# A two-layer decoder trunk on one core: low rank and decays one chunk later, pooling's sums put off behind the tile's two evacuations, three early weight splits in place of six

## The chip, the cores and the metric

The kernel runs on one core of a Trainium2 chip, in one launch. The metric is device time in microseconds (us) of that core, as the median of several runs. The kernel before has a median of 1512.12 us (1510.86, 1512.12, 1513.85).

## The reference

The input x has 2048 tokens of width 1024. Two layers follow each other; each projects x by one wide matrix, runs two groups of heads, gates them with SiLU, maps back by an output matrix, adds 1.41 x and normalises.

```python
def _even_layer(...):
    h = x @ w_in
    q, k, v, g_a, a_lr, u, sv, g_b = _split(h, EVEN_SIZES)
    log_a = jax.nn.log_sigmoid((a_lr @ w_a2 + b_a)) / GLA_TAU        # rank 16
    o = _gla(q, k, v, log_a)              # gated linear attention, 4 heads, chunks of 64
    o_a = _head_rmsnorm(o, gla_norm_g) * jax.nn.silu(g_a)
    o_b = _spatial_gating(jax.nn.gelu(u), jax.nn.gelu(sv), ...) * jax.nn.silu(g_b)
    return _layer_norm(DN_ALPHA * x + jnp.concatenate([o_a, o_b], -1) @ w_out, ln_g, ln_b)

def _odd_layer(...):
    q, k, v, g_c, p, g_d = _split(x @ w_in, ODD_SIZES)
    o = _retention(rotary(q), rotary(k), v)                         # 4 heads, chunks of 128
    o_c = _head_groupnorm(o, ret_norm_g) * jax.nn.silu(g_c)
    o_d = _multiscale_pool(p, w_pool, pool_scale) * jax.nn.silu(g_d)  # windows 2, 4, 8, 16
    return _layer_norm(DN_ALPHA * x + jnp.concatenate([o_c, o_d], -1) @ w_out, ln_g, ln_b)
```

`_multiscale_pool` takes, per group of 128 channels, the mean of the last w tokens minus the token itself, and multiplies it by a 128 x 128 matrix.

## The kernel before, in words

The tokens are worked through in four blocks of 512; each block goes through layer 0 and then layer 1, so every weight is read four times. All large products are made of fp32r pairs: `split` (L87 to L90) cuts a tile into a high part (a copy on ACT, L89) and a low part (a subtraction on DVE, L90), and each 128 x 128 weight tile is multiplied in three passes (high by high, high by low, low by high).

**Units.** `unit` computes one group of 512 output columns (or 256, 272) from eight tiles of 128 rows each (`kt`). It does two of the four outputs at a time, in two PSUM buffers of the pool `big`, which has four. So the matmuls of the second pair run while the first pair is evacuated by `evac`. A unit has 96 matmuls. The first unit of the first block alone does all four outputs at once (`width=4`).

**Weights.** SP fetches weights in order into `raw` (seven buffers); `cut` splits the next landed one into one of twelve `wt` buffers. `pace` is called after each `kt` and lets a cut through whenever its credit reaches 1.0. Where a unit needs a tile that isn't cut yet, it cuts it on the spot.

**Steps.** Work that isn't part of a unit is put in a list by `later(fn, delay)`. `between` is called four times in a unit (after a quarter of its matmuls each; here a chunk); it lowers every delay by one and runs what has reached zero, in the order of the list. The order on each engine is the order in which the program calls; nothing is moved afterwards.

**The start of a block** (`layer0`). Unit 1 gives half of v and the 16 columns of the low rank: `evac_v0` copies these to `alr` (DVE, L502 to L504) and v to `vt` (eight copies by `values`, L370 on ACT; in the first block half of them L373 on DVE). Unit 2 (256 columns) gives the rest of v. Meanwhile three steps follow one another: `low_rank` (four transposes L511, the copy `alrT` L512), `decay` (two matmuls L455, then L458 to L464 on ACT and L459 on DVE) and `decay2` (the scan and the exponentials, L471 to L485, with `f` at L522 to L524). Unit 3 gives q and k; its `evac_qk` multiplies them by the decays (L549, L550) after the first pair, and two chunks later PE transposes the keys (L555).

**Pooling** (`layer1`, `pool_unit`). Its first pair of outputs are two channel groups of p, its second pair their gates. Evacuating p copies the 16 carried tokens (L785, DVE) and the tile (L786, ACT) into `pb`, adds shifted copies (L791; one to four additions), scales (L796), saves the carry (L799) and splits the result. After the second pair, `out` multiplies it by the pooling matrix (L778, PE) in a PSUM buffer of the pool `trp`, which has two. The retention's steps (`attend`, L385 on PE; L413, L417, L733, L752 on DVE) run in the same units; their state products sit in `trp` too.

```python
later(low_rank, 1)
later(decay, 2)
later(decay2, 3)
...
pace(3 * width * cols / 512.0 if width < 4 else 0.75 * 6)
...
credit[0] = min(credit[0] + matmuls / 6.0, 2.0)
while credit[0] >= 1.0 and room[0] > hold[0] and landed:
    cut()
    credit[0] -= 1.0
```

Of the kernel before, what the change touches and what calls it, by code (L numbers as in the profile page):

```python
# [9 lines left out]
F32 = mybir.dt.float32  # L10
# [3 lines left out]
ALU = mybir.AluOpType  # L14
# [3 lines left out]
P = 128  # L18
# [3 lines left out]
TB = 512  # L22
NB = SEQ // TB
# [3 lines left out]
WINDOWS = (2, 4, 8, 16)  # L27
# [24 lines left out]
def trunk(ctx, tc, x, xT, pos, wv, w, w_a2, pvec, rowp, sgu_rows, w_sT, w_pool, ropec, poolc, out):  # L52
    nc = tc.nc
# [10 lines left out]
    pl = ctx.enter_context(tc.tile_pool(name="pl", bufs=4))  # L64
# [9 lines left out]
    def big():  # L74
        return ps_big.tile([P, 512], F32, tag="big", name="big")

    def tr():
        return ps_tr.tile([P, 4, P], F32, tag="tr", name="trp")

    def w2(name):  # L80
        return work.tile([P, TB], F32, tag="w2", name=name)

    def flat(t):
        return t.rearrange("p a b -> p (a b)")


    def split(src, hi, lo):  # L87

        nc.scalar.activation(hi, src, AF.Copy)  # L89
        nc.vector.tensor_tensor(lo, src, hi.bitcast(F32), op=ALU.subtract)  # L90
# [23 lines left out]
    def cut():  # L114
        raw, n, width = landed.pop(0)
        assert room[0] > 0
        room[0] -= 1
        t = wpool.tile([P, 2, 512], F32R, tag="w", name="wt")
        c = n * width
        split(raw[:, 0:c], t[:, 0, 0:c], t[:, 1, 0:c])  # L120
        ready.extend((t[:, :, i * width:(i + 1) * width], i == n - 1) for i in range(n))
        fetch()

    def pace(matmuls):
# [4 lines that stand above are left out]
# [9 lines left out]
    def act_unit():  # L138
        return acts.tile([P, 4, 2, TB], F32R, tag="T", name="T")
# [4 lines left out]
    def later(fn, delay=1):  # L144
        steps.append([delay, fn])

    def between():
        ready = []
        for e in steps:
            e[0] -= 1  # L150
            if e[0] <= 0:
                ready.append(e)
        for e in ready:
            steps.remove(e)
        for e in ready:
            e[1]()
# [7 lines left out]
    def unit(xs, evac, token_major, width=2, cols=512):  # L164


        wt = []
        for n in range(0, 4, width):
            ps = [big()[:, 0:cols] for _ in range(width)]
            for kt in range(KT):  # L170
                if len(wt) == kt:
                    while not ready:
                        cut()
                    wt.append(ready.pop(0))
                t, last = wt[kt]
                for i, p_ in enumerate(ps):
                    sl = slice((n + i) * P, (n + i + 1) * P)
                    xt = xs[kt // 4][:, kt % 4]
                    for q, (a, b) in enumerate(PASSES):
                        lhsT, rhs = (xt[:, a, sl], t[:, b, :]) if token_major else (t[:, a, sl], xt[:, b, :])  # L180
                        nc.tensor.matmul(p_, lhsT=lhsT, rhs=rhs, start=(kt == 0 and q == 0),  # L181
                                         stop=(kt == KT - 1 and q == 2))
                if n + width == 4 and last:
                    room[0] += 1
                pace(3 * width * cols / 512.0 if width < 4 else 0.75 * 6)
                if width > 1 and (kt + 1) % (KT // width) == 0 and kt < KT - 1:
                    between()
            for i, p_ in enumerate(ps):
                evac(n + i, p_)
            between()  # L190
# [12 lines left out]
    def gate(dst_u, h, psT, gain, sil):  # L203

        y = w2("y")
        nc.vector.scalar_tensor_tensor(y, psT, gain, sil, op0=ALU.mult, op1=ALU.mult)  # L206
        later(lambda: split(y, dst_u[:, h, 0, :], dst_u[:, h, 1, :]))

    def layer_norm_out(xs, rows, lnrow, after, cuts=1):
        ln = r8.tile([P, 2, D], F32, tag="r8", name="ln")  # L210
        for i in range(2):
            nc.sync.dma_start(ln[:, i, :], rowp[lnrow + i:lnrow + i + 1, :].broadcast_to([P, D]))
        gt, bt = ln[:, 0, :], ln[:, 1, :]
        sts = [small.tile([P, 2, 6], F32, tag="lnst", name="lnst", bufs=5) for _ in range(NT)]

        def evac(half, t, ps):
            row = rows[t // 2][:, t % 2, :]
            rh = row[:, half * 512:half * 512 + 512]
            nc.vector.scalar_tensor_tensor(rh, rh, ALPHA, ps, op0=ALU.mult, op1=ALU.add)  # L219
            nc.vector.bn_stats(sts[t][:, half, :], rh)  # L220
            if half == 1:
                mv = small.tile([P, 2], F32, tag="lnmv", name="lnmv")
                nc.vector.bn_aggr(mv, sts[t])  # L223
                rs = small.tile([P, 1], F32, tag="lnrs", name="lnrs")
                rstd(rs, mv[:, 1:2], LN_EPS)

                def scale():
                    nc.vector.scalar_tensor_tensor(row, row, mv[:, 0:1], gt, op0=ALU.subtract, op1=ALU.mult)  # L228
                    for c in range(0, D, D // cuts):
                        cs = slice(c, c + D // cuts)  # L230
                        nc.vector.scalar_tensor_tensor(row[:, cs], row[:, cs], rs, bt[:, cs],  # L231
                                                       op0=ALU.mult, op1=ALU.add)
                        after(t, row, cs)

                later(scale)

        unit(xs, lambda t, ps: evac(0, t, ps), True)
        unit(xs, lambda t, ps: evac(1, t, ps), True, width=1)
# [25 lines left out]
    carry = const.tile([P, 4, 16], F32, name="carry")  # L264
# [8 lines left out]
    poolt = const.tile([P, 4, 16], F32, name="poolt")  # L273
# [14 lines left out]
    for kt in range(KT):  # L288
# [3 lines left out]
        raw, _, width = landed.pop(0)  # L292
# [195 lines left out]
    def layer0(b, xs):  # L488
# [6 lines left out]
        def values(t, ps, s):  # L495
            by_heads(both_copy if b == 0 and s == 0 else act_copy,
                     lambda r, c: vt[half(r), t, (2 * c + s) * P:(2 * c + s + 1) * P],
                     lambda c, r: ps[half(c), r * P:(r + 1) * P])
# [29 lines left out]
        if b == 0:  # L528
            constants()
            later(constants2, 3)  # L530
            later(constants3, 4)
        later(low_rank, 1)
        later(decay, 2)
        later(decay2, 3)
        unit(xs, lambda t, ps: values(t, ps, 1), True, cols=256)


# [149 lines left out]
    def layer1(b, xs, rows):  # L687
# [76 lines left out]
        cc, cd = act_unit(), act_unit()  # L764


        def pool_unit(half):
            def evac(n, ps):
                g = 2 * half + n % 2
                slot = (g + 2) % 4  # L770
                if n >= 2:
                    sg = w2("sg")
                    nc.scalar.activation(sg, ps, AF.Silu)

                    def out():
                        pt = flat(tr())
                        for n, (i, j) in enumerate(PASSES):
                            nc.tensor.matmul(pt, lhsT=wp[:, i, g * P:(g + 1) * P], rhs=cd[:, slot, j, :],  # L778
                                             start=(n == 0), stop=(n == 2))
                        gate(cd, slot, pt, pool_s[:, g:g + 1], sg)  # L780

                    later(out, 1)
                    return
                pb = pl.tile([P, 16 + TB], F32, tag="pl", name="pb")
                nc.vector.tensor_copy(pb[:, 0:16], carry[:, g, :])  # L785
                nc.scalar.activation(pb[:, 16:], ps, AF.Copy)  # L786
                src, off, step = pb, 0, 1
                while step < WINDOWS[g]:
                    off2 = off + step
                    dst = pl.tile([P, 16 + TB], F32, tag="pl", name="pl")  # L790
                    nc.vector.tensor_tensor(dst[:, off2:], src[:, off2:], src[:, off2 - step:16 + TB - step], op=ALU.add)  # L791
                    src, off, step = dst, off2, step * 2
                if b == 0:
                    nc.gpsimd.tensor_tensor(src[:, 16:32], src[:, 16:32], poolt[:, g, :], op=ALU.mult)
                pd = w2("pd")
                nc.vector.scalar_tensor_tensor(pd, src[:, 16:], 1.0 / WINDOWS[g], pb[:, 16:],  # L796
                                               op0=ALU.mult, op1=ALU.subtract)
                if b < NB - 1:
                    nc.vector.tensor_copy(carry[:, g, :], pb[:, TB:TB + 16])  # L799

                split(pd, cd[:, slot, 0, :], cd[:, slot, 1, :])

            unit(xs, evac, False)

        pool_unit(1)
# [110 lines left out]
```

## Time and profile before

| what | value |
|---|---|
| median of 3 runs | 1512.12 us |
| the profiled execution: its time / its span | 1510.03 us / 1508.3 us |
| PE busy with matmuls | 1472.0 us, 98% of the span, 8752 matmuls |
| PE idle | 36.3 us |
| DVE busy | 985.4 us, 65% |
| ACT busy | 594.9 us, 39% |
| mean DMA traffic | 108 GB/s |
| mean granted clock of PE | 0.993 |

Of the chain that ended last, PE holds 84%, and 76% of the span is the line of the large products, L181. PE has little idle time, so what matters is where it idles, what ended each wait, and in which stretches its clock was granted at half.

### The profile page before, as it was taken

The page shows a single profiled execution, that of the slowest core. Times are in us where ns is not written, and L with a number is a line of the kernel's source. Part 1 is how long each engine was busy: PE and PEld are TensorE (multiplying, and loading weights), DVE is VectorE, ACT ScalarE, POOL GpSimd, SP SyncE. Part 2 cuts the span into 40 slices and gives each one's busy share as a digit, 9 for nine tenths or more (in the row PEclk, how much of TensorE's full clock was granted, in tenths as well). Part 3 has the DMA queues.
Part 4 walks back from the last instruction along what each step waited for, and adds up shares of the span by engine and source line. Part 5 has one row for each costly group of instructions (what it writes and reads, how often), then busy time and mean ns, then how long its engine had stood idle before and what let it go on. Part 6 is the DMA issues. An engine that isn't in the chain of part 4 may idle for free.

```text
span 1508.3 us, 23315 instructions
## 1 busy us (share of the span) xinstructions
PE 1472.0 (98%) x8752; PEld 1226.2 (81%) x8752; DVE 985.4 (65%) x2008; ACT 594.9 (39%) x1116; POOL 116.3 (8%) x185
## 2 busy tenths in 40 slices
PE   7999999999999999999999999999999999999997
PEld 6888888788878888878887888887888888888786
DVE  5596486756657458675665746867575564696655
ACT  5634324243643333434264342333427434143430
POOL 1020010100101001000100100000010010100001
PEclk9999999999999999999999999999999999999999
DMA  7324423124523341313352344232435225222321
GB/s 235 98 69 156 122 74 111 58 70 156 168 84 102 124 140 56 113 57 113 127 168 87 97 135 116 63 106 70 137 111 160 86 84 169 83 91 78 92 83 56
DMA packets 87059, 162.35 MB, mean 108 GB/s; under 512 B 10097, under 2 KB 18337, under 8 KB 86945
## 3 DMA queue, kind: packets, MB, share of 16 engines
q1 hardware_dynamic: 86944, 160.85, 34.3%
q8 instruction: 69, 1.13, 0.3%
q14 instruction: 46, 0.37, 0.1%
HBM read 152.43 MB, written 8.39 MB: 107 GB/s over the span
## 4 chain that ended last, share of the span: by engine, by line
PE 84%; DVE 6%; ACT 4%; issue 2%; DMA 1%; POOL 1%; SPq 1%; DVEq 0%; POOLq 0%; ACTq 0%
PE big L181 76%; PE att L385 3%; DVE wt L90 2%; ACT v L370 1%; DVE pl L791 1%; PE trp L778 1%; PE trp L626 1%; PE trp L678 1%; ACT wt L89 1%; PE trp L385 1%; DMA raw<-in_wv 1%; DVE ta L472 0%; SPq L109 0%; PE trp L718 0%; PE trp L814 0%
## 5 line engine op out<-in xcount | busy, mean ns | idle before, releaser
L181 PE MATMUL big<-wt,T 128*128 128x512 f32 (+2 forms) x3456 | 727.0, 370 | 10.9 <-DVE v L373 6.4
L181 PEld LDWEIGHTS big<-wt,T 128*128 128x128 f32 x3456 | 600.1, 190 | 117.8 <-ACT v L370 6.8
L181 PE MATMUL big<-T,wt 128*128 128x512 f32 x2688 | 630.6, 393 | 5.6 <-ACT v L370 5.6
L181 PEld LDWEIGHTS big<-T,wt 128*128 128x128 f32 x2688 | 501.7, 188 | 116.1 <-ACT v L370 8.6
L90 DVE TENSOR_TENSOR wt<-raw,wt 128x512 fp32r<-128x512 f32 (+1 forms) x496 | 318.0, 672 | 247.3 <-ACT wt L89 246.0
L89 ACT ACTIVATE wt<-raw 128x512 fp32r<-128x512 f32 (+1 forms) x496 | 296.3, 615 | 327.4 <-PE big L181 236.2
L219 DVE SCALAR_TENSOR_TENSOR rows<-rows,big 128x512 f32<-128x512 f32 x64 | 43.6, 681 | 59.0 <-PE big L181 59.0
L198 POOL TENSOR_SCALAR lnrs<-lnmv 128x1 f32<-128x1 f32 x32 | 33.3, 1042 | 615.8 <-DVE lnmv L223 615.8
L370 ACT ACTIVATE v<-big 64x128 f32<-64x128 f32 (+1 forms) x184 | 56.6, 308 | 35.0 <-PE big L181 17.7
L680 ACT ACTIVATE T<-trp 128x512 fp32r<-128x512 f32 x32 | 17.4, 596 | 106.5 <-PE trp L678 106.5
L231 DVE SCALAR_TENSOR_TENSOR rows<-rows,lnrs,ln 128x1024 f32<-128x1024 f32 (+1 forms) x36 | 41.6, 1165 | 19.5 <-POOL lnrs L201 18.6
L201 POOL TENSOR_TENSOR rs<-rs,neghalf 128x4 f32<-128x4 f32 x48 | 49.3, 1028 | 3.9
L220 DVE BATCH_NORM_STATS2 lnst<-rows 128x6 f32<-128x512 f32 x64 | 44.4, 694 | 2.2
L228 DVE SCALAR_TENSOR_TENSOR rows<-rows,lnmv,ln 128x1024 f32<-128x1024 f32 x32 | 41.0, 1282 | 0.9
L206 DVE SCALAR_TENSOR_TENSOR y<-trp,pv,sg 128x512 f32<-128x512 f32 x48 | 33.7, 744 | 9.5 <-PE trp L653 5.3
L786 ACT ACTIVATE pb<-big 128x512 f32<-128x512 f32 x16 | 9.4, 590 | 74.4 <-PE big L181 74.4
L89 ACT ACTIVATE T<-y 128x512 fp32r<-128x512 f32 x48 | 29.4, 627 | 23.6 <-DVE y L206 23.2
L638 ACT ACTIVATE act<-big 128x512 f32<-128x512 f32 x32 | 18.3, 596 | 51.2 <-PE big L181 50.5
L604 DVE BATCH_NORM_STATS2 st<-zt 128x6 f32<-128x128 f32 x64 | 13.6, 275 | 35.0 <-ACT zt L600 35.0
L791 DVE TENSOR_TENSOR pl<-pb 128x527 f32<-128x527 f32 x16 | 11.3, 708 | 32.6 <-ACT pb L786 31.8
L90 DVE TENSOR_TENSOR T<-y,T 128x512 fp32r<-128x512 f32 x48 | 31.6, 688 | 0.5
L744 DVE BATCH_NORM_STATS2 st<-att 128x6 f32<-128x128 f32 x64 | 14.2, 284 | 22.4 <-PE att L385 21.9
(197 smaller groups left out, 981.4 us busy)
## 6 DMA issues: line engine op xcount, KB each, us to landing
raw<-in_w SPq DMA_DIRECT2D x448, 256.0 KB, 2.9
xraw<-in_xT SPq DMA_DIRECT2D x32, 256.0 KB, 3.6
rows<-in_x SPq DMA_DIRECT2D x8, 1024.0 KB, 7.6
ln<-in_rowp SPq DMA_DIRECT2D x16, 512.0 KB, 6.1
out<-rows SPq DMA_DIRECT2D x12, 512.0 KB, 2.7
raw<-in_wv SPq DMA_DIRECT2D x32, 136.0 KB, 3.0
raw<-in_wv SPq DMA_DIRECT2D x32, 128.0 KB, 2.9
out<-rows SPq DMA_DIRECT2D x8, 256.0 KB, 2.0
```

The costliest lines, as they stand in the source:

```text
L89: nc.scalar.activation(hi, src, AF.Copy)
L90: nc.vector.tensor_tensor(lo, src, hi.bitcast(F32), op=ALU.subtract)
L181: nc.tensor.matmul(p_, lhsT=lhsT, rhs=rhs, start=(kt == 0 and q == 0), stop=(kt == KT - 1 and q == 2))
L198: nc.gpsimd.tensor_scalar(dst, var, eps, None, op0=ALU.add)
L201: nc.gpsimd.tensor_tensor(dst, dst, neghalf[:, :n], op=ALU.pow)
L206: nc.vector.scalar_tensor_tensor(y, psT, gain, sil, op0=ALU.mult, op1=ALU.mult)
L219: nc.vector.scalar_tensor_tensor(rh, rh, ALPHA, ps, op0=ALU.mult, op1=ALU.add)
L220: nc.vector.bn_stats(sts[t][:, half, :], rh)
L228: nc.vector.scalar_tensor_tensor(row, row, mv[:, 0:1], gt, op0=ALU.subtract, op1=ALU.mult)
L231: nc.vector.scalar_tensor_tensor(row[:, cs], row[:, cs], rs, bt[:, cs], op0=ALU.mult, op1=ALU.add)
L370: nc.scalar.activation(dst, src, AF.Copy)
L385: nc.tensor.matmul(dst, lhsT=lhsT, rhs=rhs, start=start, stop=stop, skip_group_check=True)
```

## The change

Three edits, word for word:

```diff
-                pace(3 * width * cols / 512.0 if width < 4 else 0.75 * 6)
+                pace(3 * width * cols / 512.0 if width < 4 else 2.4)
...
-        later(low_rank, 1)
-        later(decay, 2)
-        later(decay2, 3)
+        later(low_rank, 2)
+        later(decay, 3)
+        later(decay2, 4)
...
                 pb = pl.tile([P, 16 + TB], F32, tag="pl", name="pb")
                 nc.vector.tensor_copy(pb[:, 0:16], carry[:, g, :])
                 nc.scalar.activation(pb[:, 16:], ps, AF.Copy)
-                src, off, step = pb, 0, 1
-                while step < WINDOWS[g]:
...
-                split(pd, cd[:, slot, 0, :], cd[:, slot, 1, :])
+
+                def sums():
+                    src, off, step = pb, 0, 1
+                    while step < WINDOWS[g]:
...
+                    split(pd, cd[:, slot, 0, :], cd[:, slot, 1, :])
+
+                later(sums)
```

The body of `sums` is the old code, unchanged. In the changed file the lines of the pooling sums are two higher (L793 for L791, L798 for L796, L801 for L799), and so are those of the second transposes, L818 for L814.

How it moves instructions is shown at three places.

**ACT, start of the first block**, from the last splits ahead of unit 1's evacuation (`v` is the tile of values, `alrT` the low rank; the eight copies are those of two outputs' evacuations). Before:

```order
L89 ACTIVATE wt<-raw 128x512 x6
L370 ACTIVATE v_232<-big 64x128 x8
L89 ACTIVATE wt<-raw 128x512 x2
L512 ACTIVATE alrT<-trp 48x512
```

Now:

```order
L89 ACTIVATE wt<-raw 128x512 x3
L370 ACTIVATE v_232<-big 64x128 x8
L89 ACTIVATE wt<-raw 128x512 x4
L370 ACTIVATE v_232<-big 64x128 x8
L512 ACTIVATE alrT<-trp 48x512
L89 ACTIVATE wt<-raw 128x512 x2
L89 ACTIVATE wp<-wraw 128x512
L458 ACTIVATE ta<-trp,pv 128x512 x2
L462 ACTIVATE ta<-ta 128x512 x2
L464 ACT_TABLE_LOAD
L464 ACTIVATE ta<-ta 128x512 x2
L89 ACTIVATE wt<-raw 128x512 x2
```

Three splits stand ahead of the first evacuation in place of six, and eleven in place of twelve ahead of the exponentials; the twelfth is the eighth weight tile of unit 3.

**ACT, start of the second block**, the same steps (`G` are the scaled q and k):

```order
 L370 ACTIVATE v_3695<-big 64x128 x8
-L89 ACTIVATE wt<-raw 128x512 x2
+L89 ACTIVATE wt<-raw 128x512 x3
+L370 ACTIVATE v_3695<-big 64x128 x8
 L512 ACTIVATE alrT<-trp 48x512
-L89 ACTIVATE wt<-raw 128x512
-L370 ACTIVATE v_3695<-big 64x128 x8
+L89 ACTIVATE wt<-raw 128x512 x2
 L458 ACTIVATE ta<-trp,pv 128x512 x2
```

```order
 L89 ACTIVATE wt<-raw 128x512 x2
+L370 ACTIVATE v_3695<-big 64x128 x8
 L482 ACT_TABLE_LOAD
```

The low rank now stands behind unit 2's first evacuation and one more split, and unit 2's second evacuation has moved from behind the exponentials to ahead of them. On PE the four transposes L511 move behind 24 more matmuls, and so do the two L455.

**DVE, the pooling of two channel groups, first block** (`pb` is the tile with its carry, `pl` the sums, `pd` the result). Before:

```order
L785 COPY pb<-carry 128x16
L791 TENSOR_TENSOR pl<-pb 128x527
L791 TENSOR_TENSOR pl<-pl 128x525
L791 TENSOR_TENSOR pl<-pl 128x521
L796 SCALAR_TENSOR_TENSOR pd<-pl,pb 128x512
L799 COPY carry<-pb 128x16
L90 TENSOR_TENSOR T<-pd,T 128x512
L785 COPY pb<-carry 128x16
```

Now:

```order
L785 COPY pb<-carry 128x16 x2
L793 TENSOR_TENSOR pl<-pb 128x527
L793 TENSOR_TENSOR pl<-pl 128x525
L793 TENSOR_TENSOR pl<-pl 128x521
L798 SCALAR_TENSOR_TENSOR pd<-pl,pb 128x512
L801 COPY carry<-pb 128x16
L90 TENSOR_TENSOR T<-pd,T 128x512
```

Only the second group's carry copy has moved, ahead of the first group's sums; the sums themselves stand where they stood, since `between` follows the evacuations at once and a delay of one is then spent.

## Rows read from the trace of the kernel before

**Rows 1.** The page: span, and busy time by engine.

```profile
span 1508.3 us, 23315 instructions
...
PE 1472.0 (98%) x8752; PEld 1226.2 (81%) x8752; DVE 985.4 (65%) x2008; ACT 594.9 (39%) x1116; POOL 116.3 (8%) x185
```

**Rows 2.** What PE waited for, whole span: us in total, times, longest us.

```profile
PE trp L778 <- DVE s L417: 9.5, 4, 2.8
PE big L181 <- DVE v L373: 6.4, 2, 5.7
PE big L181 <- ACT v L370: 5.6, 6, 1.7
...
PE trp L455 <- ACT alrT L512: 1.6, 3, 0.5
```

**Rows 3.** Timeline, first block: start, us, engine, line, tiles, count, idle before.

```profile
17.74 0.69 DVE L90 TENSOR_TENSOR wt<-raw,wt 128x512 fp32r<-128x512 f32 x1 [0.79 <-ACT wt L89]
...
23.22 0.16 DVE L502 CAST alr<-big 128x16 fp32r<-128x16 f32 x1
...
25.01 0.98 PE L181 MATMUL big<-wt,T 128*128 128x256 f32 x3 [5.65 <-DVE v L373]
...
26.70 4.33 PE L181 MATMUL big<-wt,T 128*128 128x256 f32 x21 [0.71 <-DVE v L373]
...
34.90 6.01 PE L181 MATMUL big<-wt,T 128*128 128x256 f32 x48
36.30 1.26 ACT L458 ACTIVATE ta<-trp,pv 128x512 f32<-128x512 f32 x2
...
41.56 16.88 PE L181 MATMUL big<-T,wt 128*128 128x512 f32 x72
...
50.04 1.14 ACT L89 ACTIVATE wt<-raw 128x512 fp32r<-128x512 f32 x2
```

**Rows 4.** Stretch after that wait: busy by engine, granted clock, DMA share, GB/s.

```profile
25.00:30.20 5.20, 4.48 (x19) 4.22 (x20) 3.16 (x16) 2.53 (x8) 0.00 (x0) 0.50 0.70 229
```

**Rows 5.** Timeline, start of the second block.

```profile
399.32 1.16 PE L511 MATMUL trp<-ident,alr 128*48 128x128 f32 x4
...
402.06 1.15 ACT L89 ACTIVATE wt<-raw 128x512 fp32r<-128x512 f32 x2
...
403.88 0.73 PE L455 MATMUL trp<-alrT,wa 48*128 48x512 f32 x2 [0.53 <-ACT alrT L512]
...
410.40 11.07 PE L181 MATMUL big<-T,wt 128*128 128x512 f32 x48
...
421.99 2.25 ACT L370 ACTIVATE v<-big 64x128 f32<-64x128 f32 x8
422.81 0.68 DVE L549 TENSOR_TENSOR G<-big,ta 128x512 f32<-128x512 f32 x1
423.15 0.96 PE L181 MATMUL big<-T,wt 128*128 128x512 f32 x3 [1.68 <-ACT v L370]
...
429.19 0.60 PE L555 MATMUL trp<-ident,G 128*128 128x128 f32 x4
```

**Rows 6.** Timeline, pooling in the first block.

```profile
279.95 0.17 DVE L785 COPY pb<-carry 128x16 f32<-128x16 f32 x1
...
291.31 1.63 PE L778 MATMUL trp<-T,wp 128*128 128x512 f32 x6 [2.83 <-DVE s L417]
292.78 5.64 PE L181 MATMUL big<-T,wt 128*128 128x512 f32 x24
```

**Rows 7.** Timeline, the same place in the second block.

```profile
661.59 2.76 PE L778 MATMUL trp<-T,wp 128*128 128x512 f32 x6 [2.23 <-DVE s L417]
664.14 6.10 PE L181 MATMUL big<-T,wt 128*128 128x512 f32 x24
```

**Rows 8.** Stretches behind both pooling waits, columns as in rows 4.

```profile
291.30:298.30 7.00, 6.99 (x30) 5.53 (x30) 5.84 (x12) 1.78 (x4) 0.00 (x0) 1.00 0.44 134
...
661.90:665.10 3.20, 3.20 (x9) 2.46 (x9) 3.16 (x8) 0.57 (x2) 0.00 (x0) 0.50 0.00 0
```

More of the change, by code (lines that the diff above doesn't have):

```diff
@@ L786, in evac @@
                 nc.scalar.activation(pb[:, 16:], ps, AF.Copy)
-                src, off, step = pb, 0, 1
-                while step < WINDOWS[g]:
[L789 to L799, printed above, removed]
-                split(pd, cd[:, slot, 0, :], cd[:, slot, 1, :])
+                def sums():
+                    src, off, step = pb, 0, 1
+                    while step < WINDOWS[g]:
+                        off2 = off + step
+                        dst = pl.tile([P, 16 + TB], F32, tag="pl", name="pl")
+                        nc.vector.tensor_tensor(dst[:, off2:], src[:, off2:], src[:, off2 - step:16 + TB - step], op=ALU.add)
+                        src, off, step = dst, off2, step * 2
+                    if b == 0:
+                        nc.gpsimd.tensor_tensor(src[:, 16:32], src[:, 16:32], poolt[:, g, :], op=ALU.mult)
+                    pd = w2("pd")
+                    nc.vector.scalar_tensor_tensor(pd, src[:, 16:], 1.0 / WINDOWS[g], pb[:, 16:],
+                                                   op0=ALU.mult, op1=ALU.subtract)
+                    if b < NB - 1:
+                        nc.vector.tensor_copy(carry[:, g, :], pb[:, TB:TB + 16])
+                    split(pd, cd[:, slot, 0, :], cd[:, slot, 1, :])
+                later(sums)
             unit(xs, evac, False)
```

## The prediction
> **What bounds the kernel now.** I read the page first: PE is busy for 1472.0 of 1508.3 us [rows 1], so no other engine sets the time by its load, and the change, which takes no matmul away, can only earn what PE idles or runs slowly: 36.3 us of idle time, and stretches at half clock. Second, the waits of PE over the whole span [rows 2]. Four of them stand where this change moves something: the pooling matmuls behind DVE (9.5 us in four waits, one a block), the first block's second unit behind evacuation copies on DVE (6.4), q and k's second pair behind evacuation copies on ACT (5.6 in six, two in each later block), and the decay matmuls behind the low rank (1.6 in three). Third, the timeline at each of these places, to see what the releasing engine did just before. Fourth, the granted clock behind the waits, since a wait can cost more than its length.
>
> In the first block DVE finishes the third early split at 18.43 (17.74 + 0.69), but takes up the first evacuation only at 23.22, behind splits four to six; PE idles 5.65 us until 25.01 and 0.71 more until 26.70 [rows 3]. In that stretch the granted clock is 0.50, that is 1.2 of 2.4 GHz [rows 4], and 21 matmuls take 4.33 us where 48 later ones take 6.01, 0.125 us each [rows 3]. In the second block the wait for ACT is 1.68 us at 423.15: ACT frees those buffers with eight copies only from 421.99, behind the exponentials [rows 5].
>
> **Early splits.** With three, DVE is free at 18.43. The first output's last matmul should be done by then (an estimate: unit 1 ends 5.65 us before 25.01, at 19.36; the other three outputs' last nine matmuls, at some 0.15 us, come after it). So evacuation starts at about 18.45 in place of 23.22, 4.8 us earlier, and PE resumes at about 20.2, takes the second buffer at 21.9, and has idled 0.9 and 1.3 us in place of 6.36.
>
> Does the clock still fall? The nearest rows disagree. Behind a pooling wait of 2.83 us the clock stayed at 1.00, behind one of 2.23 us it was 0.50 for some three us [rows 8]. The price of a fall is 1.6 us: six and 24 matmuls took 2.76 + 6.10 in place of 1.63 + 5.64 [rows 6, 7]. For about 2.2 us of idling cut in two I take the dearer end, that it falls. The Trainium skill ("TensorE: Matmul & The Clock Gate", the two states) says that the hardware's watch on the engine runs freely and doesn't restart with the kernel, so that the same kernel shows a different number of slow matmuls from run to run; the two pooling waits agree with that, and by it this term could be 1 us better.
>
> The three splits left out are not gone; they move behind the evacuation, and the chain of the decays has to be crossed before the twelfth. At the slow clock 21 matmuls end at 26.2 (21.9 + 4.33); 24 more at 0.125 at 29.3; then eight copies (2.25, as in [rows 5]), the low rank (about 0.6, as for one split), two splits (1.15) and wp's (0.6) bring L458 to 33.9, against 36.30. From L458 to the first split behind the exponentials it was 13.74 us (36.30 to 50.04) [rows 3]; I keep that and get 47.6, and 48.2 when its high part is done. PE meanwhile: 24 matmuls 3.0, the decays' two 0.7 [rows 5], 24 more 3.0, and, as estimates, 0.4 for the transposes without their wait and 0.8 for the eight small ones of a constant bias give 37.2 for the start of q and k, against 41.56. A tile takes six matmuls of 0.234 (16.88 / 72), so the eighth is wanted at 47.0 and PE stalls for about 1.2 us, some 1.5 with its low part. The first pair ends near 49.9 in place of 52.8 (41.56 + 48 x 0.234): **minus 2.9**. At the full clock it is minus 3.9 with a stall of 2.0. The bounds are minus 4.8 (no stall) and nothing (the chain and a fallen clock eat it all).
>
> **Low rank and decays later.** In blocks two to four, the second evacuation of unit 2 now stands ahead of the exponentials on ACT. ACT gets there after about 1.2 us more of other work than before, near 415, and the buffers are free by 417.3; PE wants them at 421.4. So the wait by ACT's copies goes wholly: 5.6 us in three blocks, 1.87 each [rows 2]. What is late next? The low rank: ACT runs three splits from 402.06 (two took 1.15) to 403.8, eight copies of 2.25 to 406.0, and its own copy to 406.6. PE has its 48 matmuls and transposes behind it at 402.6, 24 more at 405.5, and waits 1.1 us at the decay matmuls where it now waits 0.53 there and about 0.6 inside the transposes, which took 1.16 for four [rows 5]. Then q and k start at about 410.35 against 410.40: nothing gained or lost. The exponentials end some 1.3 us later, but two splits have left the space between them and L549, whose start stays at 422.8; PE transposes the keys at 429.19 today [rows 5], about two us earlier then, with L550 done at 424.2 (two of 0.68). That cover is three us. **Minus 5.6**; bounds: nothing, if the low rank's wait grows by as much, and minus 7 if it shrinks too.
>
> **Pooling.** The heading of the change promises a chunk; the order shows none. The sums still stand directly behind the evacuations and ahead of the next attention step on DVE, so the state products are released as late as before and the pooling matmuls go on waiting for the second PSUM buffer. What leaves the chain is one carry copy of 0.17 us [rows 6], now under the wait for the first tile's copy on ACT: 4 x 0.17, **minus 0.7** of 9.5. The second tile's copy on ACT comes some 3.5 us earlier, which frees a buffer that nobody waits for. Bounds: nothing, and minus 1.5. POOL's multiplication in the first block and SP's queue keep their order; the eleventh weight's fetch may start three us later, and is landed long before use.
>
> **Sum.** Minus 2.9, 5.6 and 0.7 is minus 9.2 us. The profiled execution took 1510.03 us (span 1508.3 and 1.7 around it), 2.1 below the median; on it the sum gives 1500.8, and on the median of 1512.12, with the same distance, **1502.9 us**. Time gained by PE at a block's start is kept, since the later waits are not for something with a clock of its own: each follows from work that PE released.
>
> **Rivals.**
>
> *The first block gives nothing.* The stall at the eighth tile is long enough for a fall of the clock (1.6 us), and the chain is another 1.3 us slower. For: that split stands behind the whole decay chain. Against: its start moves with L458. 1512.1 - 5.6 - 0.7 = 1505.8.
>
> *The low rank becomes the wait.* In blocks two to four PE's wait at L455 grows by 1.9 us, and the clock falls behind it: 3 x 3.5 = 10.5 against the gain of 9.2, so 1513.4, no change that can be told. It decides where the low rank's copy on ACT ends after 408.5 rather than 406.6, for instance if the third split ahead of it waits for its data. Against: no split there waited for a DMA.
>
> *The clock stays up behind pooling.* Three of the four pooling waits lost it in this execution, one didn't [rows 6 to 8]. A block will be two us shorter, so the waits fall elsewhere; if none loses it, 3 x 1.6 more: 1498.1. By the Trainium skill's sentence on the free-running watch (same page) this is chance in each run; the rows, four waits, cannot contradict it.
>
> *Slower: the decays come too late for the keys.* The chain starts about three us later in PE's order; if the whole of it, and ACT's 2.25 us of copies now inside it, reaches L549, PE waits at L555 for about two us and loses the clock there, 3.6 us a block: 1502.9 + 4 x 3.6 = 1517.3. It decides from an end of L550 after some 429 in the second block; for slower than before by 3 us each wait with its clock must cost over 3 us. Against: two splits leave the chain, and my sum ends L550 at 424.2.
>
> That pooling's sums do move behind the attention's tile would be worth nearly 9.5 + 4.8 us; the order excludes it.
>
> **How the numbers follow.** A measurement of this kernel can tell about 0.2%, 3 us, from no change. Forecast 0.66 (its own range 1499.5 to 1506.0), clock stays up 0.08, first block gives nothing 0.13: faster 0.87. The low rank as the wait 0.09: same. Decays too late 0.04: slower. The range of 1497.5 to 1508.5 takes in the first three with their bounds and leaves out 0.13 and a little of the tails.
>
> **What would show it.** The first evacuation on DVE near 18.5 and PE's second unit from about 20; a wait of one to two us inside the first block's q and k, released by a split on ACT; no wait of PE for ACT's copies at q and k in later blocks, and one of about 1.1 us at L455; L778 still waiting for DVE's state sums, 2.0 to 2.7 us each. Wrong would be a new wait at L555, a low rank that ends after 408.5, or a pooling wait that is gone.

## The result and the profile after

The changed kernel takes 1497.47 us (median of 4 runs, 1496.89 to 1497.93) against 1511.49 us of the kernel before in the same series (a fourth run, 1510.23, beside the three that gave 1512.12); the ratio is 0.9905, with a 95% interval of 0.9888 to 0.9922, so it is 14.4 us faster, 11.8 to 16.9. I had forecast 9.2 us and 1502.9; the range ended at 1497.5, a hair above. The direction, the places and the order of the terms were right, the sizes too small. One run of the low-rank experiment below took 6956.62 us at a granted clock of 1.00, against 1499.37 to 1504.58 in its other five; it is left out there, and what held it up was not traced.

| what | before | after |
|---|---|---|
| profiled execution: time / span, us | 1510.03 / 1508.3 | 1497.93 / 1496.2 |
| PE idle, us | 36.3 | 27.6 |
| PE busy, us | 1472.0 | 1468.6 |
| PE waits for evacuation copies on ACT, L370 | 5.6 | none |
| PE waits for evacuation copies on DVE, L373 | 6.4 | 2.6 |
| PE waits at the pooling matmuls, L778 | 9.5 | 8.4 |
| PE waits for the low rank, L455 | 1.6 | 3.1 |

The page and PE's waits over the span, after (they answer to [rows 1, 2]):

```profile
span 1496.2 us, 23299 instructions
...
PE 1468.6 (98%) x8752; PEld 1225.9 (82%) x8752; DVE 983.5 (66%) x2008; ACT 596.3 (40%) x1116; POOL 115.9 (8%) x185
```

```profile
PE trp L778 <- DVE s L417: 8.4, 4, 2.5
PE big L181 <- ACT wt L89: 5.3, 2, 4.5
PE trp L455 <- ACT alrT L512: 3.1, 3, 1.0
PE big L181 <- DVE v L373: 2.6, 2, 1.5
```

One wait has vanished from the list, one has grown, and `ACT wt L89` has two entries: 4.5 us at the very start, which the kernel before has too, and a new one of 0.84 us at the eighth weight tile. Timeline of the first block after (against [rows 3]; start, us, engine, line, tiles, count, idle before):

```profile
17.99 0.69 DVE L90 TENSOR_TENSOR wt<-raw,wt 128x512 fp32r<-128x512 f32 x1 [0.82 <-ACT wt L89]
18.60 0.17 DVE L502 CAST alr<-big 128x16 fp32r<-128x16 f32 x1
...
20.40 0.59 PE L181 MATMUL big<-wt,T 128*128 128x256 f32 x3 [1.49 <-DVE v L373]
...
22.09 7.14 PE L181 MATMUL big<-wt,T 128*128 128x256 f32 x45 [1.09 <-DVE v L373]
...
33.23 1.24 ACT L458 ACTIVATE ta<-trp,pv 128x512 f32<-128x512 f32 x2
...
36.89 9.81 PE L181 MATMUL big<-T,wt 128*128 128x512 f32 x42
...
46.88 2.70 ACT L89 ACTIVATE wt<-raw 128x512 fp32r<-128x512 f32 x5
...
47.55 7.42 PE L181 MATMUL big<-T,wt 128*128 128x512 f32 x30 [0.84 <-ACT wt L89]
...
54.80 0.60 PE L555 MATMUL trp<-ident,G 128*128 128x128 f32 x4
```

The first evacuation follows the third split at once, PE resumes at 20.40, and q and k start at 36.89 in place of 41.56. After 42 matmuls, seven tiles of six, PE stalls until the split behind the exponentials. The keys' transposes come at 54.80 against 58.28 before (its row below): 3.5 us won.

```profile
58.28 0.60 PE L555 MATMUL trp<-ident,G 128*128 128x128 f32 x4
```

The start of the second block after (against [rows 5]):

```profile
401.60 2.25 ACT L370 ACTIVATE v<-big 64x128 f32<-64x128 f32 x8
403.87 0.59 ACT L512 ACTIVATE alrT<-trp 48x512 fp32r<-48x512 f32 x1
...
404.52 0.73 PE L455 MATMUL trp<-alrT,wa 48*128 48x512 f32 x2 [1.02 <-ACT alrT L512]
...
408.15 16.52 PE L181 MATMUL big<-T,wt 128*128 128x512 f32 x72
...
412.53 2.25 ACT L370 ACTIVATE v<-big 64x128 f32<-64x128 f32 x8
...
420.28 0.68 DVE L549 TENSOR_TENSOR G<-big,ta 128x512 f32<-128x512 f32 x1
...
424.51 0.60 PE L555 MATMUL trp<-ident,G 128*128 128x128 f32 x4
```

The second evacuation (412.53) stands ahead of the exponentials, and 72 matmuls of q and k run through where they were broken after 48. The low rank waits behind eight copies, and PE for it, 1.02 us. To compare blocks I take the distance from the last pooling matmuls of the block ahead; before and after:

```profile
339.47 1.56 PE L778 MATMUL trp<-T,wp 128*128 128x512 f32 x6
```

```profile
337.29 1.56 PE L778 MATMUL trp<-T,wp 128*128 128x512 f32 x6
```

To the keys' transposes (429.19 and 424.51) it is 89.72 us before and 87.22 after: 2.5 us won in the second block, and as much in each of the other two. The pooling waits after, first and last block, and the clock behind the first (busy by engine, granted clock, DMA share, GB/s):

```profile
287.54 2.10 PE L778 MATMUL trp<-T,wp 128*128 128x512 f32 x6 [2.54 <-DVE s L417]
...
1394.85 1.64 PE L778 MATMUL trp<-T,wp 128*128 128x512 f32 x6 [1.95 <-DVE s L417]
```

```profile
287.50:291.50 4.00, 3.96 (x11) 3.20 (x12) 3.95 (x10) 1.07 (x2) 0.00 (x0) 0.62 0.12 21
```

Each wait is 0.28 us shorter. In this execution the clock fell behind the waits of the first three blocks and not behind the fourth; before, behind the last three and not the first. Both lost it three times there, so it makes no difference between the two profiles.

The two spans differ by 12.1 us, and the landmarks give it whole: 3.5 (start) + 3 x 2.5 (low rank and decays) + 4 x 0.28 (pooling) = 12.1.

### The profile page after: what moved, and what is told of

Same layout as the page of the kernel before. It is cut to its first block, busy times and chain, and to the rows that moved or that the text cites. A ratio compares the mean times of both kernels' runs of the same rounds, so it can differ in the third digit from the quotient of the medians.

```text
span 1496.2 us, 23299 instructions
## 1 busy us (share of the span) xinstructions
PE 1468.6 (98%) x8752; PEld 1225.9 (82%) x8752; DVE 983.5 (66%) x2008; ACT 596.3 (40%) x1116; POOL 115.9 (8%) x185
## 4 chain that ended last, share of the span: by engine, by line
PE 93%; DVE 4%; ACT 1%; DMA 1%; issue 1%; POOL 0%; DVEq 0%; POOLq 0%; ACTq 0%; SPq 0%
PE big L181 84%; PE att L385 3%; DVE pl L793 1%; PE trp L778 1%; PE trp L626 1%; PE trp L678 1%; PE trp L385 1%; DVE wt L90 1%; PE trp L818 0%; PE trp L653 0%; PE trp L718 0%; DMA raw<-in_wv 0%; DMA xraw<-in_xT 0%; ACT T L89 0%; DVE pd L798 0%
## 5 line engine op out<-in xcount | busy, mean ns | idle before, releaser
L89 ACT ACTIVATE wt<-raw 128x512 fp32r<-128x512 f32 (+1 forms) x496 | 296.7, 616 | 329.0 <-PE big L181 256.4
L370 ACT ACTIVATE v<-big 64x128 f32<-64x128 f32 (+1 forms) x184 | 56.7, 308 | 36.0 <-PE big L181 19.0
L89 ACT ACTIVATE T<-y 128x512 fp32r<-128x512 f32 x48 | 29.4, 627 | 22.2 <-DVE y L206 21.8
L793 DVE TENSOR_TENSOR pl<-pb 128x527 f32<-128x527 f32 x16 | 11.3, 704 | 31.2 <-ACT pb L786 31.2
```

What stands on the lines that cost most here:

```text
L370: nc.scalar.activation(dst, src, AF.Copy)
```

## The experiments

All ratios are against the kernel before, run on the same chip in the same series (medians of 1511.0, 1511.25 and 1510.7 in three series). The first four rows are of the first series; the kernels of 1496.19, 1487.63, 1480.04 and 1523.91 us are of the second, the other four of the third. The kernel before moved by 0.55 us between series, so a smaller difference across two of them says little.

| run | median us | ratio, 95% interval |
|---|---|---|
| early splits alone | 1509.37 | 0.9982 (0.9974 to 0.9991) |
| low rank and decays alone (five runs) | 1501.13 | 0.9924 (0.9911 to 0.9938) |
| pooling's sums alone | 1510.54 | 0.9991 (0.9982 to 0.9999) |
| changed kernel, pooling matmuls a chunk later | 1483.01 | 0.9809 (0.9796 to 0.9822) |
| kernel before, pooling matmuls a chunk later | 1496.19 | 0.9896 (0.9880 to 0.9912) |
| the same, low rank and decays later | 1487.63 | 0.9841 (0.9825 to 0.9856) |
| the same, pooling's sums too | 1486.68 | 0.9832 (0.9813 to 0.9851) |
| 1483.01's kernel, low rank copied by DVE | 1480.04 | 0.9790 (0.9775 to 0.9806) |
| the same, four early splits | 1480.21 | 0.9788 (0.9769 to 0.9807) |
| the same, two early splits | 1482.37 | 0.9803 (0.9783 to 0.9823) |
| the same, three, twelfth split ahead | 1478.69 | 0.9778 (0.9759 to 0.9796) |
| changed kernel, sums really a chunk later | 1523.91 | one run |

**One edit at a time.** The first three kernels are the kernel before with one hunk of the diff each. Their gains are taken from the ratios; the medians alone give less, 1.6, 9.9 and 0.5 us.

```diff
-                pace(3 * width * cols / 512.0 if width < 4 else 0.75 * 6)
+                pace(3 * width * cols / 512.0 if width < 4 else 2.4)
```

> Only the first edit: three early splits in place of six; low rank, decays and pooling as before. Theory A (each edit has its own price, and my terms were sized too small): 3 to 5 us faster than before, all of it within the first 60 us, with PE taking up the second unit near 20.4 us. Theory B (the edits need each other): the eighth weight tile of q and k or the low rank stalls PE in the first block and less than 1.5 us is left.

Measured: 2.7 us faster (1.4 to 3.9). The evacuation starts as in the combined kernel, but in the profiled execution the clock stayed up (21 matmuls take 2.75 us where they took 4.33 before), PE reaches q and k earlier, and the weights fall behind earlier; from its timeline:

```profile
20.45 0.59 PE L181 MATMUL big<-wt,T 128*128 128x256 f32 x3 [0.94 <-DVE v L373]
22.14 2.75 PE L181 MATMUL big<-wt,T 128*128 128x256 f32 x21 [1.10 <-DVE v L373]
...
44.87 10.70 PE L181 MATMUL big<-T,wt 128*128 128x512 f32 x42 [2.05 <-ACT wt L89]
```

PE stalls 2.05 us at the sixth tile, and the keys come at 55.41, 2.9 us earlier than before. That is theory A's start and just under its 3 to 5 us; theory B's stall is there too but leaves more than its 1.5, a limit that the interval does not quite shut out.

```diff
-        later(low_rank, 1)
-        later(decay, 2)
-        later(decay2, 3)
+        later(low_rank, 2)
+        later(decay, 3)
+        later(decay2, 4)
```

> Only the second edit: low rank and decays one chunk later; six early splits. Theory A: each of the three later blocks starts 2.5 us shorter, 0.6 more than the listed wait of 1.87, since a wait shows only what comes after the last matmul has drained and each of two waits hides some 0.25 us of drain; 7.5 us faster in all, the first block unchanged within 1 us. Theory B: the extra in the combined kernel came from the first block or the clock; then about 5.6 us faster and L555 in the second block no more than 1.9 us earlier, counted from the pooling matmuls ahead of it.

Measured: 11.5 us faster by the ratio (9.4 to 13.5), 9.9 by the medians, more than either theory. From its timeline:

```profile
343.01 1.56 PE L778 MATMUL trp<-T,wp 128*128 128x512 f32 x6
...
430.24 0.60 PE L555 MATMUL trp<-ident,G 128*128 128x128 f32 x4
```

The distance is 87.23, 2.5 us shorter as theory A had it. The other two to four us can't be read there: the profile is of the longest of the five executions, 1504.58 at a mean granted clock of 0.991, where the shortest, 1499.37, had 0.996. One source of such differences shows in the profiles of the first and the third kernel, which still have the wait for ACT's copies (stretches behind it: second and third block of the first kernel, third block of the third):

```profile
423.10:429.50 6.40, 6.40 (x22) 5.10 (x23) 1.94 (x3) 1.89 (x3) 0.00 (x0) 0.75 0.28 83
795.60:803.20 7.60, 7.42 (x35) 5.83 (x34) 3.37 (x5) 4.26 (x10) 0.00 (x0) 1.00 0.46 149
...
795.60:803.20 7.60, 7.41 (x24) 5.63 (x25) 2.84 (x5) 2.96 (x7) 0.00 (x0) 0.78 0.35 111
```

In the first kernel the clock fell behind the same wait of 1.69 and 0.19 us in the second block and not in the third; in the third kernel it fell in the third block. Where it falls, the distance is 91.25 (from the first kernel's rows) in place of 89.72, 1.5 us more:

```profile
338.20 1.56 PE L778 MATMUL trp<-T,wp 128*128 128x512 f32 x6
...
429.45 0.60 PE L555 MATMUL trp<-ident,G 128*128 128x128 f32 x4
```

So a wait that costs 2.5 us where the clock stays up costs 4.0 where it falls. Four profiles have these waits (before, the first and the third kernel, and the kernel of 1496.19 below); the clock fell behind two of their twelve pairs. By that, as an estimate, three blocks lose some 0.75 us a run, so what gave the rest of this experiment's gain stays open.

```diff
+                def sums():
...
+                later(sums)
```

> Only the third edit: the sums behind both evacuations of the pooling pair. Theory A: the pooling wait shrinks by 0.28 us in each block (a carry copy with the gap around it), 1.1 us faster in all, apart from the clock, which can fall or stay behind each of the four waits at 1.6 us each. Theory B (the sums really moved by a chunk): the wait of 2.2 to 2.8 us is gone, 9 us or more faster.

Measured: 1.4 us faster (0.1 to 2.7). The waits are 2.55 us in the first block and 1.96 in the others, 0.28 less each. Theory A. The three edits apart give 2.7 + 11.5 + 1.4 = 15.6, together 14.4 (12.0 and 14.0 by the medians): within the intervals, so no need of each other shows, though one of some three us would not be seen.

**What the pooling wait is.**

```diff
                         gate(cd, slot, pt, pool_s[:, g:g + 1], sg)
 
-                    later(out, 1)
+                    later(out, 2 if half == 1 else 1)
```

> The changed kernel, with the pooling matmuls of the first pooling unit one chunk later, behind the retention's last tile, so that the state products' PSUM buffers are free when they come. Theory A (the wait is for the buffer alone, and the clock falls because of that wait): the four waits of 1.95 to 2.54 us are gone, and the stretches at half clock behind them too: 8.4 us of idling, about 1 of drain and some three falls of 1.6 us, 12 to 15 us faster than the changed kernel, near 1484. Theory B (DVE is the limit there and PE will wait for it somewhere else, or the clock falls anyway): less than 6 us faster, with a new wait on DVE in the units behind.

Measured: 1483.01, 14.5 us less than the changed kernel. PE's waits of this kernel, the whole list:

```profile
PE big L181 <- ACT wt L89: 5.4, 2, 4.6
PE trp L455 <- ACT alrT L512: 3.1, 3, 1.0
PE big L181 <- DVE v L373: 1.9, 2, 1.1
PE big L181 <- DVE wt L90: 0.7, 2, 0.5
```

No wait at L778 is left, nothing but 0.5 us behind a split at the start has come up elsewhere, and the mean granted clock of the profiled execution is 0.999: theory A. So DVE isn't the limit there; the matmuls only asked for a buffer of `trp` too early, and each such wait was paid with its idling and mostly with a stretch at 1.2 GHz.

**The edits priced without that wait.** The same edit on the kernel before, and then the change's edits on top, one by one.

> The kernel before, with only the pooling matmuls of the first pooling unit one chunk later. It prices the pooling wait by itself, and makes a base without the falls of the clock behind it. Theory A (the wait is for a PSUM buffer, and costs its idling, the drain and the clock): 9.5 us of idling, 1.2 of drain, three or four falls of 1.6: 13 to 17 us faster, near 1496. Theory B (DVE's load is the limit): under 9 us faster.

Measured: 1496.19, 15.7 us faster; theory A.

```diff
-        later(low_rank, 1)
+        later(low_rank, 2)
...
```

(with the two decays likewise)

> The previous kernel with low rank and decays one chunk later added. The difference between the two is the second edit's price where the pooling waits no longer add their chance. Theory A (2.5 us in each of three blocks, and one fall of the clock in some of those waits): 7.5 to 9.5 us faster than the previous kernel, with a spread between runs under 2 us. Theory B (the 11.5 us that the edit alone showed are its own): 11 us or more.

Measured: 1487.63, 8.6 us less than the previous kernel, with runs from 1487.13 to 1489.04: theory A.

```diff
-                pace(3 * width * cols / 512.0 if width < 4 else 2.4)
+                pace(3 * width * cols / 512.0 if width < 4 else 0.75 * 6)
```

(the kernel of 1483.01 without its early splits)

> All of the change but the early splits (six again), with the pooling matmuls one chunk later: against the kernel of 1487.63 it adds the pooling edit, and the kernel of 1483.01 adds the early splits to it. Theory A: without a pooling wait the pooling edit is worth nothing, so 1487 to 1488, and the splits are worth the 4 to 4.6 us that are left. Theory B: the pooling edit is worth its 1.1 us here too: 1486.5, and the splits 3.5.

Measured: 1486.68, by its number theory B, with 0.95 us for the pooling edit. The rows say theory A. From the first block's keys to its first pooling matmuls, first in the kernel of 1487.63, then in this one:

```profile
58.47 0.60 PE L555 MATMUL trp<-ident,G 128*128 128x128 f32 x4
...
295.07 1.66 PE L778 MATMUL trp<-T,wp 128*128 128x512 f32 x6
```

```profile
58.13 0.60 PE L555 MATMUL trp<-ident,G 128*128 128x128 f32 x4
...
294.73 1.66 PE L778 MATMUL trp<-T,wp 128*128 128x512 f32 x6
```

Both are 236.60 us: where PE doesn't wait, the pooling edit moves nothing. The two profiled executions, 1489.04 and 1486.92, differ at two other places: 0.3 us at the start, and 1.7 in the second block (88.95 against 87.23 from the last pooling matmuls to the keys), where the kernel of 1487.63 lost the clock behind a wait of 1.3 us for the low rank:

```profile
406.00:409.00 3.00, 3.00 (x16) 3.00 (x16) 1.09 (x2) 2.95 (x5) 0.00 (x0) 0.50 0.58 175
```

So nothing shows that the 0.95 between the medians is the edit's; it is within the runs' spread. The splits are worth 3.7 by the medians and 3.8 by the keys' transposes (58.13 here, 54.30 in the kernel of 1483.01). On this base the three steps add up to 8.6 + 0.95 + 3.7 = 13.2 us.

**The sums really a chunk later.**

```diff
-                later(sums)
+                later(sums, 2 if half == 1 else 1)
```

> The changed kernel with the first pooling unit's sums really one chunk later (a delay of two in the list), so that they stand behind the retention's third tile on DVE; the pooling matmuls stay where they are. Theory A (the sums then end after the matmuls want them: some 6 us of attention steps and 10 of sums on DVE, against 6 us of matmuls on PE): PE waits 9 to 12 us in each of four blocks, 25 to 45 us slower than the changed kernel. Theory B (as the change's heading would have it, the state products come free and the wait goes): 8 to 14 us faster.

Measured: 1523.91 in one run, 26.4 us over the changed kernel, the lower end of theory A, though PE's waits, which it put at 9 to 12 us a block, are 6.2. From its timeline, and from PE's waits:

```profile
284.19 0.70 DVE L793 TENSOR_TENSOR pl<-pb 128x527 f32<-128x527 f32 x1
...
288.11 1.95 PE L778 MATMUL trp<-T,wp 128*128 128x512 f32 x3 [3.36 <-ACT T L89]
...
293.35 1.95 PE L778 MATMUL trp<-T,wp 128*128 128x512 f32 x3 [3.29 <-ACT T L89]
```

```profile
PE trp L778 <- ACT T L89: 24.8, 8, 3.4
```

The sums start on DVE only behind the retention's tile, and PE now waits for each group's split result, twice a block. The wait for the buffer is gone, the wait for the data is worse, and the clock is at half for about ten us around the two waits (0.50 from 287.4 to 297.5). The edit as it was made is spared this because its sums do not move.

**The two waits that the change brought.** The low rank's copy:

```diff
-            nc.scalar.activation(alrT, flat(pa)[0:48, :], AF.Copy)
+            nc.vector.tensor_copy(alrT, flat(pa)[0:48, :])
```

> The kernel with the pooling matmuls one chunk later on top of all three edits (1483.0), and the low rank's copy out of PSUM moved from ACT, where it stands behind eight evacuation copies, to DVE. Theory A (the waits of 1.02 us at L455 in three blocks are ACT's queue): they go, with 0.2 to 0.3 us of drain each, 3 to 4 us faster, near 1479.5. Theory B (DVE's three splits ahead of the copy end no sooner): no change within 1 us.

Measured: 1480.04, 3.0 us less, the lower end of theory A. The copy and the matmuls behind it, second block:

```profile
397.41 0.68 DVE L512 CAST alrT<-trp 48x512 fp32r<-48x512 f32 x1
...
398.45 0.72 PE L455 MATMUL trp<-alrT,wa 48*128 48x512 f32 x2
```

The copy ends 0.4 us ahead of the matmuls, which wait for nothing. The number of early splits, on this kernel (`else 3.1` and `else 1.6` in place of `else 2.4`):

> The fastest kernel so far (1480.04) with four early splits in place of three. Theory A (a trade between the start and the eighth weight tile): the first evacuation 1.0 to 1.3 us later, the wait of about 0.6 and 0.4 us at the eighth tile of q and k gone: within 1 us of 1480. Theory B (only the start counts): 1.2 us slower.

> The same with two early splits. Theory A: the first evacuation starts up to 1 us earlier, but now the seventh weight tile waits for the end of the exponentials too, so PE stalls from it on, 1.4 us earlier: 0 to 1.5 us slower, near 1481. Theory B (only the start counts): 1 us faster.

Measured: 1480.21 and 1482.37. With four, PE's first wait is 2.82 us and the eighth tile is ready; with two the first wait is 0.71, but PE waits 0.45 and 1.21 us in unit 2 and then at the seventh tile. From the timelines of the two kernels:

```profile
21.49 0.82 PE L181 MATMUL big<-wt,T 128*128 128x256 f32 x3 [2.82 <-DVE v L373]
```

```profile
48.96 10.36 PE L181 MATMUL big<-T,wt 128*128 128x512 f32 x36 [1.98 <-ACT wt L89]
```

So it is the trade of theory A, with three and four equal; two is worse by somewhat more than I had thought. Its profiled execution is the longest of four (1484.61, the shortest 1481.18): it lost the clock once more behind the stall at the seventh tile (0.50 from 50.3 to 53.6). Last, the twelfth split by hand:

```diff
         def decay2():
+            if b == 0:
+                cut()
```

> The same (1480.04) with three early splits, and the twelfth split put ahead of the exponentials in the first block, so that the eighth weight tile of q and k is ready. Theory A (that wait is the split's place alone): 1.0 to 1.5 us faster, near 1478.8, with no wait of PE for a split there. Theory B (PE then waits for the keys' decays instead, which come 0.6 us later): no change.

Measured: 1478.69, 1.35 us less, the fastest of all: 0.9778 of the kernel before, 33 us by the ratio. That is theory A. PE's waits, the whole list:

```profile
PE big L181 <- ACT wt L89: 4.4, 1, 4.4
PE big L181 <- DVE v L373: 2.1, 2, 1.1
PE big L181 <- DVE wt L90: 0.2, 1, 0.2
```

What is left are the start, 4.4 us, and the two waits for unit 1's evacuation.

## Why the prediction was wrong

**Low rank and decays: the term that failed.** I took the listed waits, "5.6 us in three blocks, 1.87 each". In the profiled pair they are worth 2.5 each, 7.6 in three blocks and past my bound of minus 7, and on the base without pooling waits (the quiet base, the kernel of 1496.19) 8.6 us in all. Two things were left out.

First, the idle time of the list isn't the whole price of a wait. After the change, 72 matmuls run in 16.36 us from 408.15 to the start of the keys' transposes at 424.51, 0.227 each. By that, the 48 before should have handed over at 421.31 (410.40 + 48 x 0.227); PE resumed at 423.15, so the hole is 1.84 where the list says 1.68, and behind the three next matmuls it is 0.47 (423.83 to 424.30) where it says 0.18. The row of that second wait, before the change:

```profile
424.30 5.06 PE L181 MATMUL big<-T,wt 128*128 128x512 f32 x21 [0.18 <-ACT v L370]
```

The record of the 48 ends at 421.47 (410.40 + 11.07), 0.16 behind the 421.31 at which the next matmul could have started: matmuls overlap their neighbours, and the listed idling begins only when the last one has ended. With two waits in a block that is some 0.45 us, three times.

Second, in the sum I reckoned with the clock only at the start. The pair of waits that the edit removes can lose it as well, at 1.5 us each: the profiles of two experiments show it, the profile that I read did not. Two falls behind twelve such pairs in four profiles, some 0.75 us for three blocks as an estimate, bring the 7.6 to 8.4, near the 8.6 of the quiet base; how often it happens is not settled by so few, but that the forecast left out a cost that only some executions pay is shown. The time of the kernel before goes with the clock: in the experiments' three series its runs of 1509.6 to 1511.5 us have a mean granted clock of 0.992 or 0.993, those of 1512.2 to 1513.8 have 0.991, and those of 1514.9 to 1516.1 have 0.989 or 0.990. Which waits lose it in each of them was not traced, and low rank and decays alone still spread from 1499.37 to 1504.58. By the Trainium skill ("TensorE: Matmul & The Clock Gate", the two states) the watch on the engine runs freely, so that where a wait falls in it is a matter of the run; the runs agree, as the same wait in one execution lost the clock in one block and kept it in the next.

**Early splits.** Forecast 2.9, measured 3.5 in the profiled pair and 3.7 on the quiet base. The mechanism was right to the row: evacuation at 18.60 (18.45 forecast), PE back at 20.40 (20.2), L458 at 33.23 (33.9), the splits behind the exponentials at 46.88 (47.6), a stall at the eighth tile of 0.84 (1.2). The clock did fall, the dearer end that I took: 45 matmuls took 7.14 us, where I had reckoned 7.3. q and k start 4.7 us earlier where I had 4.4, and the stall takes 1.2 of that back where I had 1.5. That the clock fell is not certain for this start: in the profiles of the first experiment and of the kernel of 1483.01 it stayed up there.

**Pooling.** That the sums would not move, and the wait would stay, was right: 8.4 of 9.5 us are left. The term was 0.28 a block in place of 0.17: I took the copy's duration and left out the gap to the next instruction (the copy starts at 279.95, the sum behind it at 280.22).

**The waits that come.** The low rank's wait of 1.1 us was forecast and is 1.02; L549 kept its place in the block (83.3 us behind the last pooling matmuls before, 83.0 after) while the keys came 2.5 us earlier, and L555 waits for nothing. The rival in which the decays come too late had no ground; that in which the first block gives nothing neither. The rival nearest to the measured time, that the clock stays up behind pooling (1498.1), is not what happened: in the profile after, it fell behind three of the four waits, as before.

**The base.** The sum was set against the profiled execution and carried to the median by a fixed distance of 2.1 us. After the change the median lies 0.5 below the profiled execution in place of 2.1 above. So of the 5.4 us between forecast and median, 2.9 us are the three terms (12.1 against 9.2), 2.0 of that the low rank's, and 2.5 us are the base, that is, which execution happened to be profiled. Of the 14.0 us between the medians, 12.1 are accounted for row by row; the other two are the difference between an execution with few losses of the clock and a median one, which is argued from the clocks of the runs, not counted wait by wait.

## What to carry to other kernels

A wait of TensorE in a list costs more than it says: the overlap of its last matmul with the next, about 0.2 to 0.3 us here, and, in some executions only, a stretch at half clock worth 1.5; the change gave 14.4 us where my sum from the listed waits had 9.2. Look for the waits that ask too early for a buffer that another stage still holds: moving the asking step one chunk was worth 14.5 us without making any engine do less. And before trusting a change's name, see whether a delay in a list of steps is spent at once by the next call.

## What the runs showed of the hardware that I had not expected

The granted clock fell to half behind waits far shorter than the 2.2 us that I had seen: behind pairs of 1.7 and 0.2 us in two experiments (two pairs of twelve), and behind one of 1.3 us at L455 in the kernel of 1487.63, which the profile shows at 0.50 from about 406 to 409. It stayed at full behind one of 2.83 us in the kernel before. The length of a single wait doesn't tell whether the clock falls; in the profiled execution of the kernel of 1483.01, without the waits for pooling and for ACT's copies, it stayed at 1.00 from 11 us to 1478, behind the end of the last matmul, through three waits of 1.0 us for the low rank and those of the start.
